# The first MLP group in seven block products, with its weight sums on VectorE

## The chip, the cores and the metric

The kernel runs on one core of one Trainium2 chip. The metric is device time in microseconds, the median of several executions. Engines are named as in the profile: PE is TensorE's matmuls, PEld its weight loads, DVE is VectorE, ACT is ScalarE, POOL is GpSimd, SP is SyncE, which here only issues transfers.

## The reference, cut to what matters

One layer on 512 tokens of width 1024: an input projection, forgetting attention beside a gated linear recurrence, an output projection, cross-attention to 256 memory tokens, an MLP and a final norm. The change concerns the MLP with the residual ahead of it:

```python
h = h + memory_cross_attention(rmsnorm(h, norm_x_g[l]), mem_n, w_xq[l], w_xkv[l], w_xo[l])
u = rmsnorm(h, norm_ff_g[l]) @ w1[l]          # (512 x 1024) @ (1024 x 4096)
h = h + jnp.square(jax.nn.relu(u)) @ w2[l]    # (512 x 4096) @ (4096 x 1024)
...
return rmsnorm(h, final_norm_g)
```

All in float32.

## The kernel before, in words

A float32 operand is split into a rounded high half and the low remainder, and a product is three matmuls on TensorE: high by high, high by low, low by high. The high half of a weight block is a copy on ACT (L181), the low half a subtraction on DVE (L185). The residual stream lies transposed in SBUF as `hT` (four tiles of two 128-row chunks over 512 tokens); `x2_hi` and `x2_lo` are the halves of the MLP's input, the residual scaled by the norm's gain. The row scale of the norm is put in later, on the accumulators `acc` (one per 128 tokens), which get the residual back through transposes (`to_tok`: transposes on TensorE, L1258, copies on ACT and DVE, L1262 and L1264).

`residual(...)` (L1134) multiplies the cross-attention's output by `w_xo`, chunk by chunk (tile `xw`, 24 matmuls of 512 columns each): after a chunk DVE adds it into `hT` (L1157), ACT makes `x2_hi` (L1158), DVE `x2_lo` (L1159).

The MLP's width of 4096 is worked in eight groups of 512. The first weight product of a group (`u`) is a 1024 by 512 block of `w1`. Groups 1 to 7 do it in seven products in place of eight, by sums and differences of the quarters of the block and of x2 (the names "1" to "7"): `mlp_up7` (L1402), 24 matmuls of 256 columns for each product, into three PSUM banks U, Y and V. Product 1 opens U, ACT copies U to V (L1427), 5 opens Y (copied to `y5`, L1430), 6 goes on in U and ACT copies U to Y (L1432), 2 goes on in V, 7 in U, 3 in Y, 4 in U. They come in the order 1, 5, 6, 2, 7, 3, 4 (`PRODUCTS`). The sums of the weight quarters are made in DRAM by transfers that POOL issues well ahead (`sum_jobs`, with a copy on the SP queue first), paced by a count of TensorE's work (`presum.tick`), and loaded as blocks. Group 0 is done plainly: `mlp_up` (L1393), two panels of `w1` in four half loads, four banks of 24 matmuls of 512 columns. While that runs, `x_sums` (L1445) makes the differences 5, 6, 3 and 7 of x2 for the later groups, from its high and low halves.

The order on TensorE is the program's. On the other engines a scheduler orders instructions by priority and its own estimate of when they are ready; a `manual_schedule` block fixes the order of that block's instructions on the engines named, but not what falls between them. `keep_in_program_order` pins an instruction behind the one emitted before it on its engine. Buffers are shared by tags: four for weight high halves and four for low halves, two plus one for raw loads (`wr`, `t4`), twelve `s4`, four `k4`. A load waits on the SP queue for its buffer, and all loads behind it wait too; `LOADS` says how many blocks the queue runs ahead, and four blocks are split ahead.

Of the kernel before, what the change touches and what calls it, by code (L numbers as in the profile page):

```python
# [16 lines left out]
P = 128  # L17
# [29 lines left out]
def emit(  # L47
# [1083 lines left out]
    run_now(fill_rest(fill))  # L1131
    load_hT()

    def residual(src_hi, src_lo, g, dst_hi, dst_lo, name, ssq, order, nlast, after=None):  # L1134

        ps_, gens = {}, {}

        def open_(c):
            if c % 2 == 0:
                open_.wt = next_panel()  # L1140
            ps_[c] = mm(f"{name}{c}")
            gens[c] = gemm_fm(ps_[c], open_.wt, (c % 2) * P, src_hi, src_lo, order=order)

        def early():

            for c in range(3):
                open_(c)
                for _ in range(KC - nlast):
                    yield next(gens[c])

        def rest():
            for c in range(KC):
                if c not in gens:
                    open_(c)
                yield from gens[c]
                hc = hTc(c)
                ve.tensor_tensor(hc, hc, ps_[c], ALU.add)  # L1157
                ac.activation(dst_hi[:, c, :], hc, AF.Identity, scale=g[:, c : c + 1])  # L1158
                ve.scalar_tensor_tensor(dst_lo[:, c, :], hc, g[:, c : c + 1], f(dst_hi[:, c, :]), op0=ALU.mult, op1=ALU.subtract)  # L1159
# [12 lines left out]
        return early, rest  # L1172

# [79 lines left out]
    acc = []  # L1253

    def to_tok(c):
        ps = tr(f"ht{c}")
        for tb in range(NT):
            te.transpose(ps[:, tb * P : (tb + 1) * P], hTc(c)[:, tb * P : (tb + 1) * P], ident)  # L1258
        for tb in range(NT):
            d, s_ = acc[tb][:, c * P : (c + 1) * P], ps[:, tb * P : (tb + 1) * P]  # L1260
            if tb % 2 == 0:
                ac.activation(d, s_, AF.Copy)  # L1262
            else:
                ve.tensor_copy(d, s_)  # L1264

    fill.add(x_proj(1), "xq1")
    fill.run(2.0)
    for h in range(4):
        if 0 < h < 3:
            fill.add(x_proj(h + 1), f"xq{h + 1}")  # L1270
        elif h == 3:
            x2_hi, x2_lo = act_tile("x2_hi"), act_tile("x2_lo")
            early, rest = residual(o_hi, o_lo, g_ff, x2_hi, x2_lo, "xw", None, range(KC), 2, to_tok)
            fill.add(early())
        x_scores(h, 0)
        fill.run(X1)
        x_scores(h, 1)
        fill.run(X2 + X3)
        x_T_(h, 0)
        x_T_(h, 1)  # L1280
        pth, ptl = s4([2, S], f"pth{h}", R), s4([2, S], f"ptl{h}", R)
        for mc in range(2):
            ac.activation(pth[:, mc, :], xpT[h][mc], AF.Copy)
            ve.tensor_tensor(ptl[:, mc, :], xpT[h][mc], f(pth[:, mc, :]), ALU.subtract)
        if h < 3:
            fill.until(f"xq{h + 1}")
        else:
            fill.run(X4)
        x_out(h, pth, ptl)
# [1 line left out]

    run_now(fill_rest(fill))
    acc.extend(s4([D], f"acc{tb}") for tb in range(NT))
    run_now(rest())

# [3 lines left out]

    gfin = [q2p.tile([P, S], F32, tag="q2", name=f"gfin{i}") for i in range(2)]
    for i in range(2):
        gp.dma_start(gfin[i], final_norm_g[i * S : (i + 1) * S].partition_broadcast(P))
# [18 lines left out]
    def add_unit(key, shape):  # L1325
# [6 lines left out]
        def load():  # L1332
            if part == "4":
                box.append(raws.pop((kind, g)))
                return
            if part == "6":
                raw = raws[kind, g] = s4(shape, f"wr{name}")
            else:
                raw = raw_tile(name).rearrange("p (k n) -> p k n", k=shape[0])
            if part in SUMS:  # L1340
                src = wsum[kind, g, part]
            else:
                src = block(g, QUAD[part])
            dma = nc.sync.dma_start(raw, src)
            if (kind, g) == ("u", 1):
                tc.keep_in_program_order(dma)
            box.append(raw)

        def prep():
# [13 lines left out]
        unit_q.append((key, prep))  # L1363
        load_q.append(load)

    def up_units(g):
        for part in SPLITS:
            add_unit(("u", g, part), [UK, WT])
# [6 lines left out]
    def unit(*key):  # L1375
# [2 lines left out]
            unit_q.popleft()[1]()  # L1378
        got = units[key]
        at = order.index(key)  # L1380
        if key[0] == "u" and key[2] in ("5", "6"):
            at = at - 1 if key[2] == "5" else at
        while unit_q and len(order) - len(unit_q) < at + 4:
# [6 lines left out]
        ac.activation(out_, ps, AF.Relu, scale=sign)  # L1390
        ac.activation(out_, out_, AF.Square)

    def mlp_up(g, j, wt):  # L1393
        for i in range(2):
            ps = mm(f"u{g}{j}{i}")
            run_now(gemm_fm(ps, wt, i * P, x2_hi, x2_lo))
            if i == 0:
                sqs[g, j] = k4([2, S], f"sq{g}{j}")
            square(ps, sqs[g, j][:, i, :])
            yield  # L1400

    def mlp_up7(g):  # L1402

# [2 lines left out]
        h1, h2 = slice(0, HS), slice(HS, S)  # L1406
        bank = {}

        for name in PRODUCTS:
            b = {"5": "Y", "3": "Y", "2": "V"}.get(name, "U")  # L1410
            if b not in bank:
                bank[b] = (pvt if b == "Y" else mm)(f"u{b}{g}").rearrange("p (i n) -> p i n", i=2)
# [21 lines left out]
                square(ps, qa[:, :, h1])  # L1434
            elif name == "7":
                ve.tensor_tensor(qb[:, :, h2], ps, y5, ALU.add)
                square(qb[:, :, h2], qb[:, :, h2], -1.0)
            elif name == "3":
                ve.tensor_tensor(qb[:, :, h1], ps, y5, ALU.add)
                square(qb[:, :, h1], qb[:, :, h1], -1.0)  # L1440
            else:
                square(ps, qa[:, :, h2])
            yield

    def x_sums():  # L1445
# [4 lines left out]
        def part(t, k, h):  # L1450
            return t[:, k * UK : (k + 1) * UK, h * HS : (h + 1) * HS]

        blocks = {"1": (0, 0), "2": (1, 0), "2a": (0, 1), "4": (1, 1)}
        x_ = {n: (part(x2_hi, *b), part(x2_lo, *b)) for n, b in blocks.items()}
        for n in "124":
            xsum[n] = x_[n]
        names = ("5", "6", "3", "7")
        out_ = {n: tuple(t[:, i * UK : (i + 1) * UK, :] for t in (xs_hi, xs_lo)) for i, n in enumerate(names)}
        d = s4([UK, HS], "xs_d")
        for n, (a, b, sign) in (("5", ("4", "2a", -1)), ("6", (None, "1", 1)), ("3", (None, "2", -1)), ("7", ("1", "2a", -1))):  # L1460
            op = ALU.add if sign > 0 else ALU.subtract
            if a is None:
                ve.tensor_tensor(d, d, f(x_[b][0]), op)
            else:
                ve.tensor_tensor(d, f(x_[a][0]), f(x_[b][0]), op)
                ve.tensor_tensor(d, d, f(x_[a][1]), ALU.add)
            ve.tensor_tensor(d, d, f(x_[b][1]), op)
            yield
            hi, lo = out_[n]
            ac.activation(hi, d, AF.Copy, scale=-1.0 if n == "6" else 1.0)  # L1470
            if n == "6":
                ve.scalar_tensor_tensor(lo, d, -1.0, f(hi), op0=ALU.mult, op1=ALU.subtract)
            else:
                ve.tensor_tensor(lo, d, f(hi), ALU.subtract)
            xsum[n] = (hi, lo)
            yield

    def hidden_sums(g):
        qa, qb = sqs[g, 0], sqs[g, 1]
# [155 lines left out]
    def finish(tb, half):  # L1635
# [18 lines left out]
        dma_a(tb, o)  # L1654
        scale_b(tb, half, o, r, gfin[half])

    for g in range(1, NG):
        up_units(g)
        if g < NG - 1:
# [2 lines left out]
    order = [k for k, _ in unit_q]  # L1662
    xsum = {}

    def mlp_up_group(g):
        if g in SEVEN:
            yield from mlp_up7(g)
            return
        for j in range(2):
            wt = next_panel()  # L1670
            if j == 1:
                for _ in range(2):
                    unit_q.popleft()[1]()
            yield from mlp_up(g, j, wt)

    ups = mlp_up_group(0)
    next(ups)
    to_tok(KC - 2)
    to_tok(KC - 1)
    next(ups)  # L1680
    sums = x_sums()
    next(sums)
    next(sums)
    for _ in ups:
        next(sums)
        next(sums)
    ms2 = sm(NT, "ms2")
    e2 = cp.tile([P, NT], F32, name="e2")
    eps3 = cp.tile([P, NT], F32, name="eps3")
# [13 lines left out]
    scaling = scale_rows()  # L1703
    hidden_sums(0)
    for g in range(1, NG):
        for n, _ in enumerate(mlp_up_group(g)):
# [42 lines left out]
```

## Time and profile before

| | |
|---|---|
| median of 3 runs | 755.47 us (755.42 to 755.72) |
| the profiled execution | 755.52 us, of it 753.8 us from its first to its last instruction |
| PE busy | 744.8 us (99%) |
| PEld / DVE / ACT / POOL busy | 651.3 / 539.0 / 434.1 / 202.5 us |
| mean granted TensorE clock | 0.998 |
| transfers | 152.91 MB, 203 GB/s |

A row of the timeline gives the start in us, the duration in us, the engine, the line of the kernel, the operation, out<-in by the program's names (buffer numbers mostly left out), the shape and the count; in square brackets, how long the engine had stood idle and what ended that. A row of the windows gives a stretch, its length, then for each engine the busy time and the number of instructions, the granted clock, the share of the DMA engines and GB/s. The ends of matmuls are modelled; since matmuls overlap, a product's length is read from starts.

### The profile page before, as it was taken

Reading aid. Unit: us, or ns where it says so; the run is one execution under the profiler, and the core shown is the slowest. Engines: PE = TensorE matmul, PEld = TensorE weight load, DVE = VectorE, ACT = ScalarE, POOL = GpSimd, SP = SyncE. Lnnn points to the kernel's source line nnn. Section 1 sums busy time; section 2 is a strip of 40 time slices with the busy share of each in tenths; the row PEclk is TensorE's granted clock in tenths of the full one; section 3 lists DMA queues with packets and bytes.
Section 4 is the critical chain, followed back from the end, with each engine's and each line's share of the span. In section 5 each row is a group of like instructions: output and inputs, shape, how many; then the busy total and the mean of one; then the engine's idle time right before and its main releaser. Section 6 shows DMA issues by size and latency. Waiting matters only on the chain.

```text
span 753.8 us, 12203 instructions
## 1 busy us (share of the span) xinstructions
PE 744.8 (99%) x4573; PEld 651.3 (86%) x4573; DVE 539.0 (72%) x849; ACT 434.1 (58%) x721; POOL 202.5 (27%) x278
## 2 busy tenths in 40 slices
PE   9999999999999999999999999999999999999996
PEld 6889788888888988888888889898989899999985
DVE  5647873677878756645546589978788778878797
ACT  5655555655766532334434369757666757574863
POOL 7207531233433237621011211111111111100033
PEclk9999999999999999999999999999999999999999
DMA  8641987567947889985678997998989898968352
GB/s 250 197 117 56 307 264 222 179 227 254 300 175 224 269 219 210 196 164 117 128 174 156 220 209 204 224 230 240 229 205 248 221 241 210 245 194 238 125 113 111
DMA packets 109964, 152.91 MB, mean 203 GB/s; under 512 B 6177, under 2 KB 75850, under 8 KB 109906
## 3 DMA queue, kind: packets, MB, share of 16 engines
q1 hardware_dynamic: 85314, 111.74, 45.9%
q0 software_dynamic: 24000, 39.35, 30.0%
q10 hardware_dynamic: 592, 1.05, 0.4%
q8 instruction: 36, 0.59, 0.3%
q14 instruction: 22, 0.18, 0.1%
HBM read 147.91 MB, written 51.40 MB: 264 GB/s over the span
## 4 chain that ended last, share of the span: by engine, by line
PE 95%; DVE 1%; ACT 1%; POOL 1%; issue 1%; ACTq 0%; POOLq 0%
PE U L1548 4%; PE U L1549 4%; PE U L1550 4%; PE uU L1423 4%; PE uU L1422 4%; PE uU L1421 4%; PE xq L254 2%; PE wo L254 2%; PE xq L255 2%; PE xq L256 2%; PE xw L256 2%; PE xw L255 2%; PE xw L254 2%; PE wo L256 2%; PE wo L255 2%; PE Y L1548 2%
## 5 line engine op out<-in xcount | busy, mean ns | idle before, releaser
L185 DVE TENSOR_TENSOR wld<-wrd,whd 128x1024 fp32r<-128x1024 f32 x56 | 68.3, 1222 | 15.2 <-ACT whd L181 15.1
L185 DVE TENSOR_TENSOR wlu<-wru,whu 128x1024 fp32r<-128x1024 f32 x49 | 59.0, 1218 | 26.6 <-ACT whu L181 26.6
L181 ACT ACTIVATE whu<-wru 128x1024 fp32r<-128x1024 f32 x49 | 51.7, 1060 | 44.6 <-PE U L1550 16.8
L181 ACT ACTIVATE whd<-wrd 128x1024 fp32r<-128x1024 f32 x56 | 58.9, 1052 | 10.9 <-PE uU L1422 4.8
L1548 PE MATMUL U<-whd,hb 128*128 128x512 f32 x120 | 46.8, 390 | 0.0
L1549 PE MATMUL U<-wld,hb 128*128 128x512 f32 x120 | 46.8, 390 | 0.0
L1550 PE MATMUL U<-whd,hb 128*128 128x512 f32 x120 | 46.7, 389 | 0.0
L445 POOL DMA_DIRECT2D wsd<-in_w_dram x16 | 17.4, 1085 | 79.4 <-PE U L1550 15.3
L1015 POOL TENSOR_SCALAR bi<-nF,Ft 128x128 f32<-128x128 f32 (+3 forms) x32 | 21.2, 670 | 59.8 <-PE pt L1047 33.8
L445 POOL DMA_DIRECT2D wsu<-in_w_dram x14 | 17.1, 1218 | 54.6 <-PE xw L256 15.5
L1423 PE MATMUL uU<-x_hi,wlu 128*128 128x256 f32 x112 | 31.7, 283 | 0.0
L1421 PE MATMUL uY<-xs_hi,whu 128*128 128x256 f32 x112 | 31.7, 283 | 0.0
L1422 PE MATMUL uY<-xs_lo,whu 128*128 128x256 f32 x112 | 31.7, 283 | 0.0
L1423 PE MATMUL uY<-xs_hi,wlu 128*128 128x256 f32 x112 | 31.7, 283 | 0.0
L1421 PE MATMUL uU<-xs_hi,whu 128*128 128x256 f32 x112 | 31.7, 283 | 0.0
L1422 PE MATMUL uU<-xs_lo,whu 128*128 128x256 f32 x112 | 31.7, 283 | 0.0
L1423 PE MATMUL uU<-xs_hi,wlu 128*128 128x256 f32 x112 | 31.7, 283 | 0.0
L1422 PE MATMUL uU<-x_lo,whu 128*128 128x256 f32 x112 | 31.7, 283 | 0.0
L1421 PE MATMUL uU<-x_hi,whu 128*128 128x256 f32 x112 | 31.7, 283 | 0.0
L1360 POOL DMA_DIRECT2D wrd<-in_w_dram x8 | 9.7, 1218 | 78.2 <-DVE wld L185 51.1
L1360 POOL DMA_DIRECT2D wru<-in_w_dram x7 | 9.3, 1329 | 68.2 <-DVE wlu L185 68.2
L1158 ACT ACTIVATE x_hi<-hT,gv 128x512 fp32r<-128x512 f32 x16 | 11.4, 715 | 27.5 <-DVE hT L1157 27.5
(965 smaller groups left out, 2659.8 us busy)
## 6 DMA issues: line engine op xcount, KB each, us to landing
wsd<-in_w_dram SPq DMA_DIRECT2D x24, 512.0 KB, 7.5
wrd<-in_w_dram SPq DMA_DIRECT2D x24, 512.0 KB, 5.5
wrd<-wsd SPq DMA_DIRECT2D x24, 512.0 KB, 4.3
wsu<-in_w_dram SPq DMA_DIRECT2D x21, 512.0 KB, 6.1
wru<-in_w_dram SPq DMA_DIRECT2D x21, 512.0 KB, 6.2
wru<-wsu SPq DMA_DIRECT2D x21, 512.0 KB, 5.2
wsd<-in_w_dram POOLq DMA_DIRECT2D x16, 512.0 KB, 7.7
wsu<-in_w_dram POOLq DMA_DIRECT2D x14, 512.0 KB, 7.4
```

Of the source, the lines that this page charges most:

```text
L181: at = ac.activation(hi, raw, AF.Copy)
L185: ve.tensor_tensor(lo, raw, f(hi), ALU.subtract)
L254: te.matmul(ps, wh, hi, start=n_ == 0 and not begun, stop=False)
L255: te.matmul(ps, wh, lo, start=False, stop=False)
L256: at = te.matmul(ps, wl, hi, start=False, stop=k == order[-1])
L445: yield gp.dma_start(wsum[kind, g, name], src, accum_op=ALU.add, **more)
L1421: te.matmul(ps[:, i, :], whi[:, k, ws], xh[:, k, :], start=begin, stop=False, skip_group_check=True)
L1422: te.matmul(ps[:, i, :], whi[:, k, ws], xl[:, k, :], start=False, stop=False, skip_group_check=True)
L1423: at = te.matmul(ps[:, i, :], wlo[:, k, ws], xh[:, k, :], start=False, stop=k == UK - 1, skip_group_check=True)
L1548: te.matmul(ps, hi, whi[:, k, :], start=begin, stop=False, skip_group_check=True)
L1549: te.matmul(ps, hi, wlo[:, k, :], start=False, stop=False, skip_group_check=True)
L1550: at = te.matmul(ps, lo, whi[:, k, :], start=False, stop=k == 1, skip_group_check=True)
```

## The change

Group 0 is done by `mlp_up7` too, with its own order of products (`FIRST`: 1, 2, 5, 6, 7, 3, 4). The four quarters of its weight block are loaded from `w1` (`add_first`); the sums 5, 6, 7 and 4 are added up on DVE from the raw quarters (`first_sums` for three of them, the last one later). The differences of x2 are now made in float32: ACT scales the residual by the gain (`x_scaled`; in place for chunks 0 to 5, into other tiles for 6 and 7), DVE subtracts (`x_dif`, 2 instructions of 512 elements, or of 256 where chunk 6 or 7 is in it), then come a high half on ACT and a low half on DVE (`x_parts`). Three hooks in `residual` (after chunks 4, 5 and 6) begin this ahead of the MLP; the residual's last chunk is finished outside it, in a `manual_schedule` block for ACT and DVE that also holds the splits and sums of group 0. The token transposes of chunks 6 and 7 stand between products 1 and 2, their copies after product 3. In groups 0 and 1 the relu-square of products 7 and 3 is one DVE instruction in place of two on ACT (`square_neg`). The first loads of group 1 are tied behind the first group's loads on the SP queue.

```diff
-    for j in range(2):
-        specs.append(panel(w1, j * WT))
...
+                if open_end and c == KC - 1:
+                    last_xw.append(ps_[c])
+                    return
...
+                hooks.get(c, lambda: None)()
...
+    FIRST = ("1", "2", "5", "6", "7", "3", "4")
...
+    def add_first(part):
...
+        def load():
+            if rc is None or rc == "11":
+                if copies:
+                    tc.keep_in_program_order(copies.popleft()())
...
+            if rc[1] == "0":
+                raw = wrp.tile([P, D], F32, tag="wr", name=f"wr{name}", padded_shape=[P, UK * UW])
+                raw = raw.rearrange("p (k n) -> p k n", k=UK)
+            else:
+                raw = s4([UK, WT], f"wr{name}")
+            first_dma.append(nc.sync.dma_start(raw, block1(0, rc)))
+            blk[rc] = raw
...
+    def first_sums():
+
+        t5, t6 = (s4([UK, WT], f"wr0{n}") for n in "56")
+        tc.keep_in_program_order(ve.tensor_tensor(t5, blk["00"], blk["01"], ALU.add))
+        ve.tensor_tensor(blk["01"], blk["01"], blk["11"], ALU.add)
+        ve.tensor_tensor(t6, t5, blk["11"], ALU.add)
+        block_sum.update({"5": t5, "6": t6, "7": blk["01"], "4": t6})
...
-    def mlp_up(g, j, wt):
-        for i in range(2):
-            ps = mm(f"u{g}{j}{i}")
-            run_now(gemm_fm(ps, wt, i * P, x2_hi, x2_lo))
...
+    def square_neg(g, q):
+        if g < 2:
+            ve.scalar_tensor_tensor(q, q, 0.0, q, op0=ALU.min, op1=ALU.mult)
+        else:
+            square(q, q, -1.0)
...
-        for name in PRODUCTS:
+        for name in PRODUCTS if g else FIRST:
...
+        ac.activation(x67[c] if c > 5 else hTc(c), hTc(c), AF.Identity, scale=g_ff[:, c : c + 1])
...
+    def at4():
...
+        for c in range(4):
+            x_scaled(c)
+        xd["7"] = k4([UK, HS], "xd7")
+        x_dif("7", (0, h1), (0, h2), ALU.subtract, range(4))
+
+    def at5():
+        split_first("1")
+        split_first("2")
+
+    def at6():
+        first_sums()
+        x_scaled(4)
+        x_scaled(5)
+        xd["5"] = xd["6"] = xd["3"] = k4([UK, HS], "xd5")
+        x_dif("5", (4, h2), (0, h2), ALU.subtract, range(2))
+
+    first_hooks.update({4: at4, 5: at5, 6: at6})
...
+    with tc.manual_schedule(engines={mybir.EngineType.Activation, mybir.EngineType.DVE}):
+        c = KC - 1
+        x_scaled(c - 1)
+        ve.tensor_tensor(hTc(c), hTc(c), last_xw[0], ALU.add)
+        split_first("5")
+        ac.activation(x2_hi[:, c, :], hTc(c), AF.Identity, scale=g_ff[:, c : c + 1])
+        x_scaled(c)
+        ve.scalar_tensor_tensor(x2_lo[:, c, :], hTc(c), g_ff[:, c : c + 1], f(x2_hi[:, c, :]), op0=ALU.mult, op1=ALU.subtract)
+        x_dif("5", (4, h2), (0, h2), ALU.subtract, range(2, 4))
+        next(ups)
+        toks = [tok_T(c) for c in (KC - 2, KC - 1)]
+        x_parts("5")
+        x_dif("6", None, (0, h1), ALU.add, range(4))
+        split_first("6")
+        x_hi_of("7")
+        x_parts("6")
+        x_lo_of("7")
+        next(ups)
+        split_first("7")
+        next(ups)
+        split_first("3")
+        x_dif("3", None, (4, h1), ALU.subtract, range(4))
+        next(ups)
+        x_parts("3")
+        next(ups)
+        ve.tensor_tensor(block_sum["4"], block_sum["4"], blk["10"], ALU.add)
+        split_first("4")
+        next(ups)
+        for c, ps in zip((KC - 2, KC - 1), toks):
+            tok_copy(c, ps)
+        next(ups)
...
-    for _ in ups:
-        next(sums)
-        next(sums)
...
+        for n, _ in enumerate(mlp_up7(g)):
             hidden_ahead((g - 1, PRODUCTS[0]), min(n, HB))
             if g == 1:
-                next(sums, None)
                 next(scaling, None)
```

More of the change, by code (lines that the diff above doesn't have):

```diff
@@ L1132, in emit, with residual @@
     load_hT()
-    def residual(src_hi, src_lo, g, dst_hi, dst_lo, name, ssq, order, nlast, after=None):
+    def residual(src_hi, src_lo, g, dst_hi, dst_lo, name, ssq, order, nlast, after=None, hooks={}, open_end=False):
         ps_, gens = {}, {}
@@ L1255, in to_tok, with tok_T @@
     def to_tok(c):
+        tok_copy(c, tok_T(c))
+    def tok_T(c):
         ps = tr(f"ht{c}")
@@ L1272, in emit @@
             x2_hi, x2_lo = act_tile("x2_hi"), act_tile("x2_lo")
-            early, rest = residual(o_hi, o_lo, g_ff, x2_hi, x2_lo, "xw", None, range(KC), 2, to_tok)
+            early, rest = residual(o_hi, o_lo, g_ff, x2_hi, x2_lo, "xw", None, range(KC), 2, to_tok, first_hooks, True)
             fill.add(early())
@@ L1346, in load @@
                 tc.keep_in_program_order(dma)
+                order_only = mybir.DependencyInfo(mybir.DependencyClass.NoSync, mybir.DependencyReason.DATA)
+                tc.add_manual_dep(dma.ins, first_dma[-1].ins.name, order_only, reason="first group first")
             box.append(raw)
@@ L1364, in add_unit, with split_first @@
         load_q.append(load)
+    blk, block_sum, first_dma = {}, {}, []
+    def add_first(part):
+        name = f"u0{part}"
+        rc = {"1": "00", "2": "10", "5": "01", "6": "11"}.get(part)
+        def load():
+            if rc is None or rc == "11":
+                if copies:
+                    tc.keep_in_program_order(copies.popleft()())
+            if rc is None:
+                return
+            if rc[1] == "0":
[5 more added lines that the diff above has]
+            blk[rc] = raw
+        unit_q.append((("u", 0, part), None))
+        load_q.append(load)
+    def split_first(part):
+        unit_q.popleft()
+        unit_ = new_parts([UK, WT], f"u0{part}")
+        raw = block_sum[part] if part in block_sum else blk[{"1": "00", "2": "10", "3": "11"}[part]]
+        split_of(unit_[0], unit_[1], raw)()
+        units["u", 0, part] = unit_
+    def first_sums():
[4 more added lines that the diff above has]
+        block_sum.update({"5": t5, "6": t6, "7": blk["01"], "4": t6})
     def up_units(g):
@@ L1380, in unit @@
         at = order.index(key)
+        if key[:2] == ("u", 0):
+            while load_q and len(order) - len(load_q) < at + LOADS:
+                load_q.popleft()()
+            return got
         if key[0] == "u" and key[2] in ("5", "6"):
@@ L1443, in mlp_up7, with x_scaled, x_view, x_dif @@
             yield
-    def x_sums():
+    xd, x67 = {}, {}
+    h1, h2 = slice(0, HS), slice(HS, S)
+    def x_scaled(c):
+        if c > 5:
+            x67[c] = t2(f"xg{c}")
+        ac.activation(x67[c] if c > 5 else hTc(c), hTc(c), AF.Identity, scale=g_ff[:, c : c + 1])
+    def x_view(c, n, h):
+        if c > 5:
+            return x67[c][:, h].unsqueeze(1)
+        return hT[c // 2][:, c % 2 : c % 2 + n, h]
+    def x_dif(name, first, second, op, chunks):
+        t = xd[name]
+        for c in chunks[::2]:
+            n = 1 if 6 in (c + second[0], c + (first or second)[0]) else 2
+            for i in range(0, 2, n):
+                o = t[:, c + i : c + i + n, :]
+                a = o if first is None else x_view(c + i + first[0], n, first[1])
+                ve.tensor_tensor(o, a, x_view(c + i + second[0], n, second[1]), op)
@@ L1447, in x_sums, with x_blocks, part @@
+    def x_blocks():
+        def part(t, k, h):
+            return t[:, k * UK : (k + 1) * UK, h * HS : (h + 1) * HS]
+        for n, b in (("1", (0, 0)), ("2", (1, 0)), ("4", (1, 1))):
+            xsum[n] = (part(x2_hi, *b), part(x2_lo, *b))
         xs_hi, xs_lo = act_tile("xs_hi"), act_tile("xs_lo")
         xs_hi, xs_lo = (t.rearrange("p k (h n) -> p (k h) n", h=2) for t in (xs_hi, xs_lo))
-        def part(t, k, h):
-            return t[:, k * UK : (k + 1) * UK, h * HS : (h + 1) * HS]
-        blocks = {"1": (0, 0), "2": (1, 0), "2a": (0, 1), "4": (1, 1)}
@@ L1454, in x_sums @@
[L1454 to L1476, printed above, removed]
+        for i, n in enumerate("5637"):
+            xsum[n] = tuple(t[:, i * UK : (i + 1) * UK, :] for t in (xs_hi, xs_lo))
@@ L1478, in hidden_sums, with x_hi_of, x_parts, x_lo_of @@
+    def x_hi_of(n):
+        ac.activation(xsum[n][0], xd[n], AF.Copy, scale=-1.0 if n == "6" else 1.0)
+    def x_parts(n):
+        x_hi_of(n)
+        x_lo_of(n)
+    def x_lo_of(n):
+        d = xd[n]
+        hi, lo = xsum[n]
+        if n == "6":
+            ve.scalar_tensor_tensor(lo, d, -1.0, f(hi), op0=ALU.mult, op1=ALU.subtract)
+        else:
+            ve.tensor_tensor(lo, d, f(hi), ALU.subtract)
     def hidden_sums(g):
@@ L1655, in finish @@
         scale_b(tb, half, o, r, gfin[half])
+    for part in FIRST:
+        add_first(part)
     for g in range(1, NG):
@@ L1663, in emit @@
     xsum = {}
[L1665 to L1681, printed above, removed]
-    next(sums)
-    next(sums)
-    for _ in ups:
-        next(sums)
-        next(sums)
+    def at4():
+        while load_q and len(unit_q) - len(load_q) < 4:
+            load_q.popleft()()
+        for c in range(4):
+            x_scaled(c)
+        xd["7"] = k4([UK, HS], "xd7")
+        x_dif("7", (0, h1), (0, h2), ALU.subtract, range(4))
@@ new lines, in at5 @@
+    def at5():
[8 more added lines that the diff above has]
+    first_hooks.update({4: at4, 5: at5, 6: at6})
+    run_now(rest())
+    gfin = [q2p.tile([P, S], F32, tag="q2", name=f"gfin{i}") for i in range(2)]
+    for i in range(2):
+        gp.dma_start(gfin[i], final_norm_g[i * S : (i + 1) * S].partition_broadcast(P))
@@ new lines, in emit @@
+    x_blocks()
+    ups = mlp_up7(0)
+    with tc.manual_schedule(engines={mybir.EngineType.Activation, mybir.EngineType.DVE}):
[29 more added lines that the diff above has]
+        next(ups)
+        for _ in ups:
+            pass
```

16 lines of the change are left out of this document (5 added, 11 removed).

## The prediction

> **What bounds the kernel now.** I read the page's busy times first, then the chain that ended last, then who waited for whom on TensorE.
>
> ```profile
> span 753.8 us, 12203 instructions
> PE 744.8 (99%) x4573; PEld 651.3 (86%) x4573; DVE 539.0 (72%) x849; ACT 434.1 (58%) x721; POOL 202.5 (27%) x278
> PE 95%; DVE 1%; ACT 1%; POOL 1%; issue 1%; ACTq 0%; POOLq 0%
> PE warm L366 <- DVE ones L370: 1.3, 1, 1.3
> PE pt L1047 <- DVE bi L1039: 0.7, 1, 0.7
> ```
>
> TensorE (PE) is busy 99% of the span and is 95% of the chain. The last two rows are all of its waits: 2.0 us, none of them in the MLP. So the kernel is a TensorE stream without holes, and the change can win only by making that stream shorter; every hole that it opens is paid in full. The profiled execution took 755.52 us (span 753.8), 0.05 above the median of 755.47.
>
> The next view cuts that stream in two, with TensorE's busy time: the first MLP group as it is (four full products over 512 columns), and the second group, which is computed in seven products already. Behind it stand single rows of the same stretch.
>
> ```profile
> 430.34:453.02 22.68, 22.68 (x106) 1.00 0.91 192
> 453.02:473.17 20.15, 20.15 (x169) 1.00 0.73 215
> 435.79 1.04 PE L1258 MATMUL ht<-ident,hT 128*128 128x128 f32 x8
> 436.58 0.48 PE L254 MATMUL u<-x_hi,wh34a 128*128 128x512 f32 x1
> 453.02 0.28 PE L1421 MATMUL uU<-x_hi,whu 128*128 128x256 f32 x1
> 455.89 0.28 PE L1421 MATMUL uY<-xs_hi,whu 128*128 128x256 f32 x1
> ```
>
> The first group lasts 22.68 us, of which the eight transposes (435.79 to 436.58) are 0.79. One product of 24 matmuls goes from 453.02 to 455.89: 2.87 us, 0.1196 a matmul.
>
> **The change on TensorE.** 96 matmuls of 512 columns (22.68 - 0.79 = 21.89 us) become 168 of 256 (20.15 by the second row): -1.74 us. The transposes stay. That is all that can be won, and it needs no new hole anywhere.
>
> A place where the skill differs: the Trainium skill, "TensorE: Matmul & The Clock Gate" (Wait — 56ns, not 53.3ns?), gives warm matmuls N / 2.4 GHz + 2.5 ns start to start, 109.2 ns for 256 columns and 215.8 for 512; an estimate from the Trainium skill's two figures is 96 x 0.2158 - 168 x 0.1092 = 2.37 us won, 0.63 more than by the rows. Here 256 columns take 119.6 ns; the trace disagrees with the Trainium skill and decides, and the sum goes by 1.74.
>
> **What the new order asks of ACT and DVE.** The seven products come as 1, 2, 5, 6, 7, 3, 4. Their moving operands and weights are now made while they run, in an order written by hand. The prices, first DVE, then ACT (with the matmul that the last ACT row waits for):
>
> ```profile
> 424.19 0.69 DVE L1157 TENSOR_TENSOR hT<-hT,xw 128x512 f32<-128x512 f32 x1 [2.64 <-PE xw L256]
> 427.17 0.29 DVE L1264 COPY acc<-ht 128x128 f32<-128x128 f32 x1 [0.34 <-ACT acc L1262]
> 430.54 0.69 DVE L1157 TENSOR_TENSOR hT<-hT,xw 128x512 f32<-128x512 f32 x1 [0.58 <-PE xw L256]
> 432.60 0.75 DVE L1159 SCALAR_TENSOR_TENSOR x_lo<-hT,gv,x_hi 128x512 fp32r<-128x512 f32 x1
> 433.26 1.22 DVE L1465 TENSOR_TENSOR xs_d<-x_hi 128x1024 f32<-128x1024 f32 x1
> 438.66 1.23 DVE L1474 TENSOR_TENSOR xs_lo<-xs_d,xs_hi 128x1024 fp32r<-128x1024 f32 x1 [0.63 <-ACT xs_hi L1470]
> 441.13 1.22 DVE L185 TENSOR_TENSOR wlu<-wru,whu 128x1024 fp32r<-128x1024 f32 x1
> 442.27 1.22 DVE L1467 TENSOR_TENSOR xs_d<-xs_d,x_lo 128x1024 f32<-128x1024 f32 x1
> 460.20 0.68 DVE L1484 TENSOR_TENSOR s<-n,sq 128x512 f32<-128x512 f32 x1
> 460.80 0.68 DVE L1485 TENSOR_TENSOR s<-sq 128x512 f32<-128x512 f32 x1
> 745.51 0.42 DVE L1598 TENSOR_TENSOR acc<-Z,acc 128x256 f32<-128x256 f32 x1
> 437.56 1.06 ACT L1470 ACTIVATE xs_hi<-xs_d 128x1024 fp32r<-128x1024 f32 x1
> 456.80 0.58 ACT L1427 ACTIVATE uV<-uU 128x512 f32<-128x512 f32 x1
> 462.80 0.59 ACT L1432 ACTIVATE uY<-uU 128x512 f32<-128x512 f32 x1
> 435.55 0.40 PE L256 MATMUL u<-x_hi,wl34b 128*128 128x512 f32 x1
> 435.99 0.60 ACT L1390 ACTIVATE sq<-u 128x512 f32<-128x512 f32 x1 [3.95 <-PE u L256]
> ```
>
> Start to start, DVE needs 1.14 us for 1024 elements (441.13 to 442.27), 0.60 for 512, 0.66 for the low half of x2; 256 elements take 0.42. A high half of 1024 on ACT takes 1.06. Between engines pass some 0.05 us (xs_hi ends at 438.62, xs_lo starts at 438.66). ACT starts on a finished bank 0.04 us after the modelled end of the last matmul (435.95 to 435.99); for 256 columns that end is 0.28 after the matmul's start.
>
> DVE, walked through. The block sums are pinned behind the token copies of chunk 5 (427.17 + 0.29 = 427.46; by 0.06 of overlap, 427.40). Then, in emission order: three block sums (3 x 1.14), half of x2's difference 5 (0.60), the residual of chunk 7 (0.60, so 431.42 and not 430.54, hidden under product 1), weights' low half 5 (1.14), x2_lo of chunk 7 (0.66), two quarters of difference 5 (0.84): 434.66. ACT makes the high half of 5 until 435.75, and DVE stands still. Low half of 5 at 435.80, difference 6 (2 x 0.60), weights 6: free at 439.28; ACT's high half of 6 ends at 439.32, so low half of 6 from 439.36 to 440.58. Low half of 7, weights 7, weights 3 (to 443.92), difference 3 (ends 445.20), ACT's high half of 3 (to 446.30), low half of 3 from 446.35 to 447.57. Then the add after product 7 and the new DVE square (0.60 each), the fourth block sum (448.69 to 449.91), ACT's high half of weights 4 (to 451.01), its low half (to 452.27).
>
> TensorE against that:
> - Product 1 from 430.34 to 433.21, transposes to 434.00. The copy U to V (last matmul ends 433.37, + 0.04 + 0.59 = 434.00) lies under the transposes: a hole of 0.05. Without them it would cost 0.84.
> - Product 2 to 436.92, product 5 to 439.79: its low half is there at 436.95 to 437.02. Hole 0.
> - Product 6: the second matmul waits for 440.58 + 0.05: hole 0.72. Ends 443.38, modelled 443.54.
> - Product 7 writes the bank U that ACT is still copying to Y (L1432). Before, product 2 (2.87 us) stood between them and hid that; now nothing does: 443.58 + 0.59 + 0.05 = 444.22, hole 0.84. Ends 447.09.
> - Product 3: second matmul waits for low half 3: 447.62, hole 0.41. Ends 450.37.
> - Product 4: high half at 451.06 (0.69), low half, wanted by its third matmul, at 452.32 (1.14). Then 22 x 0.1196: ends 454.95.
>
> Holes: 0.05 + 0.72 + 0.84 + 0.41 + 0.69 + 1.14 = 3.85. The first group ends at 454.95 instead of 453.02, so +1.93, and nothing later gives it back, because TensorE has no slack there. **The sum: 755.52 + 1.93 = 757.45, and 757.4 beside the median.**
>
> Bounds of the two unseen things. The wait of product 7 for the copy is nowhere in this trace: 0 if some other work fell between, 0.84 by the rows above; the emission order leaves nothing between, so 0.84. DVE's order is written only relative to itself: the scheduler may put the second group's weight splits between (1.14 each) or in the four idle stretches of about 1.1 (0): I take 0, and up to 2.3 for the range.
>
> **What else moves.** The loads:
>
> ```profile
> 418.62 0.50 SPq L1344 DMA_DIRECT2D wru<-in_w_dram  x1
> 432.71 0.38 SPq L1344 DMA_DIRECT2D wru<-in_w_dram  x1
> DMA to landing us min/median/max: 6.1/6.1/7.5
> 440.00:453.00 13.00, 13.00 (x59) 10.76 (x58) 10.94 (x11) 9.32 (x15) 2.31 (x2) 1.00 0.88 173
> 453.00:473.00 20.00, 20.00 (x168) 19.98 (x167) 17.56 (x21) 20.00 (x29) 2.95 (x4) 1.00 0.72 214
> ```
>
> The same 2 MB of w1 are loaded, from the SP queue. The second group's first load, at 418.62 before, must now wait behind the first group's four and for a buffer of the 12 (four residual pairs, four accumulators, two blocks and two sums fill them), the first of which comes free with the sum t5 near 433.2. With 7.5 us to land it is there by 441; its product starts at 454.95: hidden with 11 us to spare after 2.3 of splitting. The load behind the block `10`, held until the fourth sum at 449.9, delays product 3 of the second group's raw weights to 458; wanted near 469. The stream's own count for the sums of later weights in DRAM drops by 2.6 us, so they are issued that much later; no wait of TensorE in the MLP hangs on them now, so I take 0 (at most 2.6, once).
>
> In the second group the windows (PE, PEld, DVE, ACT, POOL) show ACT busy 20.00 of 20.00 and DVE 17.56. The change takes four squares on ACT (4 x 0.6) and two high halves from there; it adds the token copies of chunks 6 and 7, moved behind product 3, and the row squares that wait for them. About even: 0, with 0 to +1.0 for the range.
>
> **Rivals.**
> - A, forecast: DVE's chain ends product 4: +1.9, 757.4.
> - B, the other side: DVE keeps up and only the copy's hole of 0.84 and the 0.05 remain: 1.74 - 0.89 = 0.85 won, 754.6. It decides if the low half of weights 4 ends by some 449.6 instead of 452.27; for it speaks that DVE idles 2.64 us ahead of 424.19 and over 3 in the hand order, against it that the sums are pinned at 427.4 and the rest is in fixed order.
> - C: no hole at all: 753.7. It needs the copy hidden, against the emission order.
> - D: two or more splits of the second group, or a late load, fall into DVE's chain (2 x 1.14) and ACT in the second group lags: +1.9 + 2.3 + up to 1.0 = 4.2 to 5.2, around 760. For it: ACT is full there; against it: the idle stretches would take them.
>
> **How the numbers follow.** A 0.47, B 0.32, C 0.04, D 0.17. Some 0.2% (1.5 us) is what a measurement of this kernel tells from no change. Of A (757.0 to 758.2 by itself, down to 756.5 if a hand-over or a block sum is cheaper) a fifth lies within 0.2%. The range reaches from B, with 0.2 for a cheaper copy, to the lower end of D: 754.4 to 759.6; C and the upper half of D are left out. Faster by over 0.2% is C and the edge of B, 0.05; within it the rest of B and that part of A, 0.41; slower 0.54.
>
> **What would show it.** In the new profile: 168 matmuls of 256 columns at 0.12 us in group 0; TensorE waiting for the Y copy once, near 0.8 us, ahead of product 7; waits for DVE's low halves ahead of products 6, 3 and above all 4, near 1.1; DVE busy nearly without a gap from 427 to 452; the first group ending near 455. If TensorE shows only the copy's wait, B is right and my DVE walk is too long; if a wait falls in the second group, D.

## The result, and the profile after

The changed kernel takes 757.81 us (median of 7 runs, 757.52 to 758.4) against 755.42 for the kernel before (7 runs): a ratio of 1.0034, 95% interval 1.0024 to 1.0045. It is 2.4 us slower; 757.4 was forecast. The profiled execution took 758.4 us, with a span of 756.7.

The page of the changed kernel, and all the waits of TensorE that the profile shows in it (engine, line, what it waited for; us in total, times, longest):

```profile
span 756.7 us, 12373 instructions
PE 745.0 (98%) x4645; PEld 653.9 (86%) x4645; DVE 544.1 (72%) x862; ACT 439.6 (58%) x727; POOL 200.7 (27%) x278
PE 91%; DVE 4%; ACT 2%; issue 1%; POOL 1%; ACTq 0%; POOLq 0%
PE warm L364 <- DVE ones L368: 1.3, 1, 1.3
PE uU L1472 <- DVE wlu L183: 0.8, 1, 0.8
PE uU L1470 <- ACT uY L1481: 0.7, 1, 0.7
PE pt L1045 <- DVE bi L1037: 0.7, 1, 0.7
PE uU L1470 <- ACT whu L179: 0.5, 1, 0.5
PE uU L1471 <- DVE xs_lo L1542: 0.5, 1, 0.5
PE uY L1471 <- DVE xs_lo L1544: 0.2, 1, 0.2
```

Two waits became seven, and the five new ones are the five that the prediction walked through: the low half of operand 6 (L1542), the copy of U to Y ahead of product 7 (L1481), the low half of operand 3 (L1544), and the high and low halves of weights 4 (L179, L183). A sixth hole, which the walk put at 0.05 us ahead of product 2, is not named as a wait, but the rows show it. DVE now makes 4% of the chain that ended last.

Next, TensorE's timeline of the changed kernel around these holes, and the start of the group (start, duration, engine, line, operation). The rows directly ahead of a wait show its length from start to start.

```profile
430.64 0.28 PE L1470 MATMUL uU<-x_hi,whu 128*128 128x256 f32 x1
...
433.51 1.04 PE L1263 MATMUL ht<-ident,hT 128*128 128x128 f32 x8
434.51 0.39 PE L1470 MATMUL uV<-x_hi,whu 128*128 128x256 f32 x1
434.74 0.28 PE L1471 MATMUL uV<-x_lo,whu 128*128 128x256 f32 x1
...
440.37 0.28 PE L1470 MATMUL uU<-xs_hi,whu 128*128 128x256 f32 x1
441.16 0.39 PE L1471 MATMUL uU<-xs_lo,whu 128*128 128x256 f32 x1 [0.51 <-DVE xs_lo L1542]
441.38 0.28 PE L1472 MATMUL uU<-xs_hi,wlu 128*128 128x256 f32 x1
...
443.90 0.28 PE L1472 MATMUL uU<-xs_hi,wlu 128*128 128x256 f32 x1
444.91 0.39 PE L1470 MATMUL uU<-xs_hi,whu 128*128 128x256 f32 x1 [0.73 <-ACT uY L1481]
...
447.88 0.28 PE L1470 MATMUL uY<-xs_hi,whu 128*128 128x256 f32 x1
448.31 0.38 PE L1471 MATMUL uY<-xs_lo,whu 128*128 128x256 f32 x1 [0.15 <-DVE xs_lo L1544]
...
451.04 0.28 PE L1472 MATMUL uY<-xs_hi,wlu 128*128 128x256 f32 x1
451.87 0.39 PE L1470 MATMUL uU<-x_hi,whu 128*128 128x256 f32 x1 [0.55 <-ACT whu L179]
452.09 0.28 PE L1471 MATMUL uU<-x_lo,whu 128*128 128x256 f32 x1
453.13 0.39 PE L1472 MATMUL uU<-x_hi,wlu 128*128 128x256 f32 x1 [0.76 <-DVE wlu L183]
453.35 0.28 PE L1470 MATMUL uU<-x_hi,whu 128*128 128x256 f32 x1
...
455.87 0.28 PE L1470 MATMUL uU<-x_hi,whu 128*128 128x256 f32 x1
```

Matmuls of 256 columns start 0.12 apart. Ahead of product 7 it is 1.01 (443.90 to 444.91), ahead of product 4's third matmul 1.04 (452.09 to 453.13). From the transposes to product 2 it is 1.00 (433.51 to 434.51), where the eight transposes took 0.79 before: a hole of 0.21. The eight triplets of product 4 end with the one at 455.51, so group 1 begins at 455.87: the first group lasts 25.23 us instead of 22.68, 2.55 more. The windows of the two groups in the changed kernel, as in the prediction (PE, PEld, DVE, ACT, POOL; the first row ends one matmul early):

```profile
430.64:455.75 25.11, 22.41 (x177) 21.19 (x175) 22.24 (x29) 15.81 (x21) 2.89 (x3) 1.00 0.74 196
455.87:476.03 20.16, 20.16 (x171) 20.16 (x169) 16.14 (x22) 20.03 (x32) 2.88 (x5) 1.00 0.91 227
```

DVE is busy 22.24 of 25.11 us in the first group; the second group takes 20.16 us, where it took 20.15. From there to the end of the MLP TensorE's rows show no further hole over 0.05 us, so the first group is where the time is lost.

### The profile page after: what moved, and what is told of

Its sections match the earlier page's. It is cut to its first block, busy times and chain, and to the rows that moved or that the text cites. A ratio compares the mean times of both kernels' runs of the same rounds, so it can differ in the third digit from the quotient of the medians.

```text
span 756.7 us, 12373 instructions
## 1 busy us (share of the span) xinstructions
PE 745.0 (98%) x4645; PEld 653.9 (86%) x4645; DVE 544.1 (72%) x862; ACT 439.6 (58%) x727; POOL 200.7 (27%) x278
## 4 chain that ended last, share of the span: by engine, by line
PE 91%; DVE 4%; ACT 2%; issue 1%; POOL 1%; ACTq 0%; POOLq 0%
PE uU L1472 4%; PE uU L1471 4%; PE uU L1470 4%; PE U L1616 4%; PE U L1617 4%; PE U L1618 4%; PE xq L252 2%; PE wo L252 2%; PE xq L253 2%; PE xq L254 2%; PE wo L253 2%; PE Y L1616 2%; PE Y L1618 2%; PE Y L1617 2%; PE wo L254 2%; PE uY L1472 2%
## 5 line engine op out<-in xcount | busy, mean ns | idle before, releaser
L183 DVE TENSOR_TENSOR wlu<-wru,whu 128x1024 fp32r<-128x1024 f32 x53 | 63.9, 1225 | 25.6 <-ACT whu L179 25.5
L179 ACT ACTIVATE whu<-wru 128x1024 fp32r<-128x1024 f32 x53 | 55.6, 1058 | 42.7 <-PE U L1618 16.8
L183 DVE TENSOR_TENSOR wld<-wrd,whd 128x1024 fp32r<-128x1024 f32 x56 | 68.5, 1225 | 13.9 <-ACT whd L179 13.9
L179 ACT ACTIVATE whd<-wrd 128x1024 fp32r<-128x1024 f32 x56 | 59.0, 1053 | 13.0 <-PE uU L1471 5.3
L1472 PE MATMUL uU<-x_hi,wlu 128*128 128x256 f32 x128 | 36.3, 284 | 0.8 <-DVE wlu L183 0.8
L1470 PE MATMUL uU<-xs_hi,whu 128*128 128x256 f32 x128 | 36.3, 284 | 0.7 <-ACT uY L1481 0.7
L1470 PE MATMUL uU<-x_hi,whu 128*128 128x256 f32 x128 | 36.3, 284 | 0.5 <-ACT whu L179 0.5
L1471 PE MATMUL uU<-xs_lo,whu 128*128 128x256 f32 x128 | 36.3, 284 | 0.5 <-DVE xs_lo L1542 0.5
L1471 PE MATMUL uY<-xs_lo,whu 128*128 128x256 f32 x128 | 36.3, 284 | 0.2 <-DVE xs_lo L1544 0.2
L1471 PE MATMUL uU<-x_lo,whu 128*128 128x256 f32 x128 | 36.2, 283 | 0.0
L1472 PE MATMUL uU<-xs_hi,wlu 128*128 128x256 f32 x128 | 36.2, 283 | 0.0
L1470 PE MATMUL uY<-xs_hi,whu 128*128 128x256 f32 x128 | 36.2, 283 | 0.0
L1618 PEld LDWEIGHTS U<-whd,hb 128*128 128x128 f32 x120 | 22.5, 188 | 4.8
L1616 PEld LDWEIGHTS U<-whd,hb 128*128 128x128 f32 x120 | 22.6, 188 | 4.5
```

What stands on the lines that cost most here:

```text
L179: at = ac.activation(hi, raw, AF.Copy)
L183: ve.tensor_tensor(lo, raw, f(hi), ALU.subtract)
L1470: te.matmul(ps[:, i, :], whi[:, k, ws], xh[:, k, :], start=begin, stop=False, skip_group_check=True)
L1471: te.matmul(ps[:, i, :], whi[:, k, ws], xl[:, k, :], start=False, stop=False, skip_group_check=True)
L1472: at = te.matmul(ps[:, i, :], wlo[:, k, ws], xh[:, k, :], start=False, stop=k == UK - 1, skip_group_check=True)
L1616: te.matmul(ps, hi, whi[:, k, :], start=begin, stop=False, skip_group_check=True)
```

## The experiments

Each kernel is the changed one with the edit shown, unless it says otherwise. Theory: DVE's chain, which starts late, sets the holes ahead of products 6, 3 and 4, and the copy of U makes the one ahead of 7. Rivals: the holes belong to the hand-overs and the fixed order wherever the sums stand; or ACT, not DVE, is the engine without room.

**The block sums earlier.**

```diff
     def at5():
         split_first("1")
         split_first("2")
+        first_sums()

     def at6():
-        first_sums()
```

> Edit: the three block sums on VectorE are issued after chunk 5 of the residual instead of after chunk 6, where VectorE stands idle. Theory (VectorE's chain sets the holes ahead of products 6, 3 and 4): the chain begins with the last residual chunk at 430.9 instead of 431.9, 1.0 us earlier; the hole at product 6 (0.67) closes, that at 3 shrinks, the low half of weights 4 comes 1.0 earlier; the copy's hole ahead of product 7 stays near 0.9. Total 757.8 - 1.0 = 756.8. Rival (the holes come from the hand-overs and the fixed order, wherever the sums stand): unchanged, 757.8.

757.18 us, ratio 1.0022 (1.0013 to 1.0030) to the kernel before, where the changed kernel has 1.0034. The profiled run's span is 754.8 against 756.7. TensorE's waits in it:

```profile
PE uU L1472 <- DVE wlu L183: 0.8, 1, 0.8
PE uU L1470 <- ACT uY L1481: 0.7, 1, 0.7
PE uU L1470 <- ACT whu L179: 0.5, 1, 0.5
```

The medians, from two sessions, differ by 0.6 us; in the trace the first group takes 24.31 us (429.69 to 454.00) instead of 25.23. That is 0.92 less, and 1.0 was expected. Gone are operand 6's wait with its restart and most of the hole behind the transposes (0.83 in place of 1.00). The wait at the copy and the two at product 4 stand as they did. So does operand 3's, which the list doesn't name: 0.43 from start to start (446.02 to 446.45), as in the changed kernel, though it was expected to shrink. TensorE comes to product 4 earlier by as much as DVE does, and the fourth sum with its hand-overs stayed in the way.

**The fourth block sum early too.** On top of the edit before.

```diff
     def at6():
+        tc.keep_in_program_order(ve.tensor_tensor(blk["10"], blk["10"], block_sum["6"], ALU.add))
...
-        ve.tensor_tensor(block_sum["4"], block_sum["4"], blk["10"], ALU.add)
         split_first("4")
```

with `block_sum["4"]` now `blk["10"]`.

> Edit: as the run before, and the fourth block sum too is made ahead of the MLP, into the raw block 10, instead of between product 7's square and the split of block 4. Theory (VectorE's chain): the sum and the hand-over to ScalarE and back leave the end of the chain, so product 4 finds its weights ready; left are the copy's hole of 0.9 to 1.0 ahead of product 7, 0.2 at each of products 2 and 3: the first group lasts 22.4 us, total 755.1, level with before. Rival (hand-overs): product 4 still waits for ScalarE and VectorE around 1 us each, 757 to 757.8.

755.23 us, ratio 0.9999 (0.9990 to 1.0008): level with before, as the theory said to 0.1 us; the first group takes 22.51 us (430.66 to 453.17), 22.4 was expected. Left in TensorE's waits:

```profile
PE uU L1470 <- ACT uY L1481: 0.7, 1, 0.7
PE uY L1471 <- DVE xs_lo L1544: 0.2, 1, 0.2
```

So moving four additions of 1.2 us, without dropping any, takes back the whole loss. The rival, by which the holes stay wherever the sums stand, falls. The run doesn't tell the fourth sum's own time from the wait for ACT that stood behind it (1.12 us on DVE in the changed kernel): both left the end of the chain together.

**The squares back on ACT, in groups 0 and 1.**

```diff
     def square_neg(g, q):
-        if g < 2:
+        if g < 0:
```

> Edit: the relu-squares of products 7 and 3 in groups 0 and 1 go back to two ScalarE instructions. Theory (VectorE's chain): one VectorE instruction of 0.6 leaves the chain ahead of the fourth sum, the last hole shrinks by it: 757.2. Group 1 gives nothing, since TensorE waits nowhere there. Rival (ScalarE is the full engine in groups 0 and 1): four more pairs of ScalarE instructions push weight splits back, 758 to 759.

759.31 us, ratio 1.0049 (1.0037 to 1.0062): a miss. The trace shows two effects of opposite sign. Group 0 did get shorter: groups 0 and 1 together take 44.76 us (first matmul of group 0 to first of the down products, 430.30 to 475.06) instead of 45.39 (430.64 to 476.03). But after that three holes open, two of them in the down products (in TensorE's rows below, then DVE's rows that lead to the first) and a short one in group 2 (0.48 from start to start, 498.52 to 499.00):

```profile
475.06 0.40 PE L1616 MATMUL U<-whd,hb 128*128 128x512 f32 x1
...
486.84 0.47 PE L1616 MATMUL U<-whd,hb 128*128 128x512 f32 x1 [0.71 <-DVE acc L1584]
492.70 0.47 PE L1616 MATMUL U<-whd,hb 128*128 128x512 f32 x1 [0.16 <-ACT hb L1565]
```

```profile
478.32 1.23 DVE L183 TENSOR_TENSOR wld<-wrd,whd 128x1024 fp32r<-128x1024 f32 x1 [1.81 <-ACT whd L179]
486.01 1.28 DVE L1584 SCALAR_TENSOR_TENSOR acc<-U,acc 128x512 f32<-128x512 f32 x2
```

ACT, full through group 1 (20.03 of 20.16 us in the changed kernel), gives the high halves of the down weights late. DVE stands idle 1.81 us for one and is then behind with the add that frees bank U. My expectation failed because I read "TensorE waits nowhere in group 1" as room on ACT.

**The squares back on ACT in group 0 alone.** `if g == 1` in that line.

> Edit: only group 0's relu-squares of products 7 and 3 go back to ScalarE; group 1 keeps its on VectorE. After the run with both groups on ScalarE: groups 0 and 1 together shortened there by 0.63 us (from 45.39 to 44.76), but holes of 1.10 and 0.55 opened in group 0's down products, behind a VectorE add that waited for ScalarE's backlog. Theory (group 1 is where ScalarE has no room, group 0's chain on VectorE is still the setter): 757.8 - 0.6 = 757.2, and no hole after the first group. Rival (any ScalarE instruction moved into either group costs): the later holes come back, 758.5 to 759.3.

757.49 us, ratio 1.0030 (1.0019 to 1.0041): 0.3 under the changed kernel's 757.81, in the direction forecast, though the intervals overlap. The trace carries the verdict: groups 0 and 1 together take 44.78 us (430.21 to 474.99) instead of 45.39, the 0.6 that was expected. The waits are the changed kernel's, less the one for the high half of weights 4 (operand 3's step of 0.42, 447.47 to 447.89, is there, though the list leaves it out),

```profile
PE uU L1472 <- DVE wlu L183: 0.8, 1, 0.8
PE uU L1470 <- ACT uY L1481: 0.7, 1, 0.7
PE uU L1471 <- DVE xs_lo L1542: 0.5, 1, 0.5
```

and no wait in the down products. One step of 0.28 in place of 0.12 is left in group 2 (497.05 to 497.33). It was group 1's squares that had no room on ACT.

**One part alone: group 1's squares on DVE, in the kernel before.** The line `square(qb[...], qb[...], -1.0)` of products 7 and 3 becomes `square_neg` as in the change.

> The kernel before with one part of the change alone: in group 1 the relu-squares of products 7 and 3 as one VectorE instruction each. Theory: TensorE waits for neither engine there in the kernel before, so nothing: 755.4 within 0.3. Rival (ScalarE is full in group 1 and the change's gain there is real): 754.8 or less.

755.34 us against 755.42, ratio 1.0002 (0.9993 to 1.0012): nothing. By itself this part is worth nothing; with the new group 0 in front it keeps ACT from falling behind, as the two runs before this one show. That this is so because the token copies and row squares come later there is argued, not shown. That ACT is full does not tell by itself: in the kernel before it is busy for all of group 1's 20.15 us, and no hole follows.

**The transposes between products 6 and 7.**

```diff
         next(ups)
-        toks = [tok_T(c) for c in (KC - 2, KC - 1)]
         x_parts("5")
...
         next(ups)
+        toks = [tok_T(c) for c in (KC - 2, KC - 1)]
         x_parts("3")
```

> Edit: the eight token transposes stand between products 6 and 7 instead of between 1 and 2. Theory: only one of the two copies of bank U can lie under the transposes; a hole of 0.85 to 0.95 opens ahead of product 2, that ahead of product 7 goes, and the end is VectorE's as before: 757.8 within 0.2. Rival (the wait ahead of product 7 is not the copy but something later): the wait at 7 stays and one at 2 is added, 758.7.

757.78 us, ratio 1.0033 (1.0020 to 1.0045): unchanged. The wait moved from one copy to the other, and the rest stayed within 0.02 us (product 7 follows the transposes with a hole of 0.11):

```profile
433.91 0.39 PE L1470 MATMUL uV<-x_hi,whu 128*128 128x256 f32 x1 [0.83 <-ACT uV L1476]
```

The matmul before it started at 432.79, so 1.12 start to start, a hole of 1.00. A copy of a bank that the next product needs cost TensorE 0.89 us in the changed kernel and 1.00 here, each with 0.10 for the restart behind it; with the transposes in between, a hole of 0.21 was left of it there and of 0.11 here.

**Product 3 ahead of 7.** On the kernel with all four sums early: order 1, 2, 5, 6, 3, 7, 4, and product 3 in a bank of its own. The diff is cut; splits and operands move as the expectation says.

```diff
-    FIRST = ("1", "2", "5", "6", "7", "3", "4")
+    FIRST = ("1", "2", "5", "6", "3", "7", "4")
...
             elif name == "6":
-                copyY[g] = ac.activation(bank["Y"], ps, AF.Copy)
+                if g == 0:
+                    y56 = t2("y56", F32, (2, HS))
+                    ve.tensor_tensor(y56, ps, y5, ALU.add)
+                else:
+                    copyY[g] = ac.activation(bank["Y"], ps, AF.Copy)
...
-                ve.tensor_tensor(qb[:, :, h1], ps, y5, ALU.add)
+                ve.tensor_tensor(qb[:, :, h1], ps, y5 if g else y56, ALU.add)
```

> Edit: on the run with all four block sums early, the products go 1, 2, 5, 6, 3, 7, 4; product 3 opens its own bank, and VectorE writes the sum of bank U after product 6 and y5 into a tile that is added to product 3, in place of ScalarE's copy of U to Y. So product 3 stands between 6 and 7 and covers the read of U; the weights' low half of 6 moves into VectorE's idle stretch ahead of operand 5, difference 3 gets a tile of its own and operand 3 comes before operand 7. Theory: the hole of about 1.0 ahead of product 7 goes and no other one over 0.3 opens; the first group lasts 21.3 us instead of 22.7: 755.3 - 1.4 = 753.9. Rival (VectorE can't have operand 3 one product earlier): holes of 0.5 to 1.0 ahead of products 6 and 3, 754.8 to 755.5.

754.99 us, ratio 0.9995 (0.9987 to 1.0004), not clear of before. The hole ahead of 7 is gone and operand 3 is in time, but I had overlooked that product 4 now follows 7 in bank U, which DVE must read first:

```profile
449.30 0.36 PE L1475 MATMUL uU<-x_hi,whu 128*128 128x256 f32 x1 [0.94 <-DVE sq L1494]
```

From the matmul ahead of it (448.08) that is 1.22.

**Group 1's first product between 7 and 4.** On the kernel of the run before: `next(ups1)`, with `ups1 = mlp_up7(1)`, stands ahead of the last product of group 0.

> Edit: on the run with product 3 ahead of 7, the first product of group 1 (its operand and its weights are there by then) is put between products 7 and 4 of group 0, so that VectorE's read of bank U after product 7 lies under it; the token copies and product 4's square leave the hand-ordered block. Theory (that run lost what it won at the Y copy to the new read of U ahead of product 4, 1.22 start to start in place of 0.12): the hole goes, 755.0 - 1.1 = 753.9, and the first two groups together take 41.4 us. Rival (group 1's weights or its later products come too late when it starts a product earlier): a hole opens in group 1, 755 or more.

756.20 us, ratio 1.0013 (1.0004 to 1.0022): worse. One hole replaced the other; group 1's first product wants the low half of its weights, which the scheduler put behind product 7's add on DVE:

```profile
450.86 0.39 PE L1477 MATMUL uU<-x_hi,wlu 128*128 128x256 f32 x1 [1.73 <-DVE wlu L183]
```

```profile
448.99 0.68 DVE L1494 TENSOR_TENSOR sq<-uU,y 128x512 f32<-128x512 f32 x1
449.59 1.21 DVE L183 TENSOR_TENSOR wlu<-wru,whu 128x1024 fp32r<-128x1024 f32 x1
```

**Those weights in the hand order.** On the kernel of the run before.

```diff
         split_first("7")
+        split_first("4")
+        unit_q.popleft()[1]()
         next(ups)
-        split_first("4")
         next(ups)
     ups1 = mlp_up7(1)
```

> Edit: as the run before, and the splits of block 4 and of group 1's first block stand ahead of product 3's add in the hand order, where VectorE has its idle stretch. Theory (the one hole left there, 2.01 start to start in place of 0.12, is the low half of group 1's first block, which the scheduler put behind product 7's add): the hole closes, 756.2 - 1.9 = 754.3, TensorE waits nowhere in the MLP. Rival (VectorE is full: what is pulled ahead pushes something else late): another hole of 1 or more, 755.3 or above.

754.15 us, ratio 0.9985 (0.9976 to 0.9994): faster than both kernels, 1.1 us under before. TensorE's waits are down to the two of the kernel before, and the first of the down products, which ends groups 0 and 1, stands at 471.89:

```profile
PE warm L364 <- DVE ones L368: 1.3, 1, 1.3
PE pt L1045 <- DVE bi L1037: 0.7, 1, 0.7
430.44 0.28 PE L1475 MATMUL uU<-x_hi,whu 128*128 128x256 f32 x1
471.89 0.40 PE L1626 MATMUL U<-whd,hb 128*128 128x512 f32 x1
```

That is 41.45 us for the two groups, where the kernel before takes 22.68 + 20.15 = 42.83: 1.38 of the 1.74 that the seven products can give. The other 0.36 are two holes too short for the list, 0.08 behind the transposes and 0.07 at product 6's second matmul, with a restart of 0.10 and 0.11 behind them.

## Why the prediction was right

- **What carries it.** The range, 754.4 to 759.6, would have held most outcomes, rival B's too. What bears the forecast out is that TensorE waits at the five places that were named, for the instructions that were named, and that the holes have about their sizes.
- **The gain of 1.74 us on TensorE** is real: the last run gets 1.38 of it, and its two short holes with their restarts are the rest. The rival C (no hole) was out of reach of this order, in which product 7 follows 6 in bank U. Another order with earlier sums came near it: 754.15 against its 753.7.
- **The copy's hole.** Predicted 0.84, in the trace 0.89 beyond the normal step (1.01 - 0.12). Moving the transposes moved it to the other copy, where it cost 1.00; the prediction had 0.84 for that. With the transposes ahead of it product 2 had 0.05 and measured 0.21. In the changed kernel ACT starts the copy at 433.88, not 0.04 after the modelled end of the last matmul (433.67) but 0.21, behind the scaling of chunk 7. In the first experiment, where ACT was idle by then, the hole is 0.04.
- **DVE's chain.** The holes, predicted and measured (start to start, less 0.12): product 6 0.72 and 0.67; product 3 0.41 and 0.31 (447.88 to 448.31); product 4's first matmul 0.69 and 0.71, its third 1.02 and 0.92. The prediction lists this last one as 1.14, but it takes one step off where two lie between (451.06 to 452.32, less 2 x 0.12, is 1.02); so its list adds up to 3.73 and not 3.85. The +1.93 is not touched, since it comes from the end of the walk at 454.95. All six holes measure 3.71 together. That the total agrees so well is partly luck, since the single ones are off by up to 0.16, both ways. That DVE's place in time was the cause is shown by the two runs with the sums early; the second of them is close to rival B, at 755.23 where that had 754.6: product 3's hole is left, and the restarts.
- **The size: +1.93 predicted, +2.55 in the trace.** Since the holes add up as walked, the 0.62 between these two figures is a term that the prediction had at nothing: TensorE's first matmul after a hole takes 0.22 to the next start instead of 0.12 (441.16 to 441.38, 453.13 to 453.35), six times in the group. But most of these restarts only use up time in which TensorE would have waited for DVE further on. Read by what ends the group, DVE is late and one restart follows. Counted from the group's first matmul, the low half of weights 4 starts at 21.21 us (451.85 - 430.64) where the walk had 20.71 (451.05 - 430.34): 0.50 late, and the restart after it is 0.10. DVE's timeline of the changed kernel:

```profile
428.40 1.22 DVE L1409 TENSOR_TENSOR wr<-wru,wru 128x1024 f32<-128x1024 f32 x1
431.93 0.68 DVE L1764 TENSOR_TENSOR hT<-hT,xw 128x512 f32<-128x512 f32 x1
...
448.18 0.68 DVE L1485 TENSOR_TENSOR sq<-uU,y 128x512 f32<-128x512 f32 x1
448.90 0.69 DVE L1447 SCALAR_TENSOR_TENSOR sq<-sq 128x512 f32<-128x512 f32 x1
449.50 1.22 DVE L1786 TENSOR_TENSOR wr<-wr,wru 128x1024 f32<-128x1024 f32 x1
451.85 1.23 DVE L183 TENSOR_TENSOR wlu<-wr,whu 128x1024 fp32r<-128x1024 f32 x1 [1.12 <-ACT whu L179]
```

  The block sums start at 428.40, 0.70 later in the same count than the walk had them. Ahead of them DVE had waited 0.93 us for x2's high half of chunk 6 (until 426.47), which ACT now makes behind a scaling (425.11); the walk took its start over from the kernel before, where that wait was 0.44. Half of difference 5, which the walk put behind the sums, is done before them and gives 0.60 back, so the add of chunk 7 is 0.21 late (1.29 us into the group, 1.08 in the walk). By the add after product 7 it is 0.39 (17.54 against 17.15). The square adds 0.12: it starts 0.72 after the add whose result it squares, while the fourth sum starts 0.60 after the square, which it does not read. The walk priced every instruction at the pitch of independent ones.
- **ACT in group 1** was put at 0, with 0 to +1.0. In the change as made it is 0 (group 1 takes 20.16). It stays 0 only because the squares left ACT there: with group 1's put back, the down products gain steps of 1.10 and 0.55 from start to start where 0.23 is the rule (485.74 to 486.84, 492.15 to 492.70). So the judgement "about even" was right, and the square on DVE was a needed part of it.
- **Rival D** did not happen: what the scheduler put between on DVE (a hidden half at 445.82, 0.69 long) fell into an idle stretch, and no late load shows in TensorE's waits.

## What to carry to other kernels

When a stream on one engine has no holes, a change that shortens it by 8% of a stage is decided by the engines that feed it: write their instructions out in order with the trace's durations, including the hand-overs, and look for idle time ahead of the stage into which preparation can be moved before counting any gain. An order of products has to be checked bank by bank: each read of an accumulator between two products needs other work on TensorE to lie under it, and swapping two products here only moved the uncovered read. An engine that nobody waits for may still be full; what it has no room for shows up a stage later and on another engine.

## What was not expected of the hardware

In these traces a TensorE stream that had waited took about 0.10 us to get back into step: 0.22 between the first two starts in place of 0.12 for 256 columns, after a wait of 1.73 us as after holes under 0.1 (0.17 to 0.23 in all). It is not the wait alone: in the kernel before the first matmul behind the eight transposes takes 0.32 (436.58 to 436.90) in place of 0.23 for 512 columns, and nothing is waited for there. What causes it stays open. In group 0 of the changed kernel it happens six times, 0.62 us beside 3.71 us of holes, though all but the last stand ahead of a wait that ends only when DVE does, so they cost nothing extra. And on DVE an instruction that reads its predecessor's result started 0.12 us later than one that doesn't (0.72 against 0.60 at 512 elements).
